# Seven half-size products in place of eight in the up projection of a SwiGLU layer, and full-height second products in the mixer

## The chip, the core and the metric

The kernel runs on one core of a Trainium2 chip. The metric is the device time of one launch in microseconds (us). The core has a matrix engine (PE, with its weight loads shown as PEld), three engines for vectors (DVE, ACT, POOL) and 16 DMA engines fed from queues, of which SP's carries nearly all weight loads here.

## The reference, cut to what matters

Two layers, each a half-step feed-forward layer, a mixer (attention, a gated linear recurrence and RWKV-7, merged by gates) and a second feed-forward layer, all in float32 with 512 tokens of 1024 channels; `D_FF` is 2816.

```python
def _swiglu(h, w_up, w_down):
    u, gte = _split(h @ w_up, [D_FF, D_FF])
    return (jax.nn.silu(u) * gte) @ w_down

for l in range(DEPTH):
    ...
    y = 0.5 * g1[:, None, :] * _swiglu(h, ffn_up[l, 0], ffn_down[l, 0])
    ...
    y = g2[:, None, :] * _mixer(h, w_in[l], ...)
    ...
    y = 0.5 * g3[:, None, :] * _swiglu(h, ffn_up[l, 1], ffn_down[l, 1])
```

## The kernel before

**Numbers.** PE multiplies in the type fp32r. To keep float32 accuracy every operand is held as two fp32r tiles, `hi` (a copy rounded to fp32r, made by ACT) and `lo` (the rest, made by a subtraction), and each product is three: hi·hi, hi·lo and lo·hi (`mm3`, lines 201 to 203). `split_w` (line 187) makes the two tiles of a weight, 128x1024 a time: ACT at line 194, and the subtraction at line 196 on DVE, or on POOL where `on_pool` is set (in the mixers, and in the first chunk of every feed-forward layer but the first). The activations of a layer lie split in `hhi` and `hlo` (1024 channels as 8 blocks `k` of 128, by 512 tokens).

**A feed-forward layer** (`ffn`, line 458) goes through the 2816 hidden channels in 22 blocks of 128, in chunks of 4, 4, 4, 5 and 5 blocks (`CHUNKS`). For a block it loads 128 columns of the u half and 128 of the gate half, splits both, and multiplies: 2 halves x 8 `k` x 3 = 48 products of 128x512 into two PSUM banks. `up_act` (line 477) then takes silu(u) on ACT, multiplies by the gate half on DVE (line 480) and splits the result (`split_act`: ACT line 649, DVE line 650). After the blocks of a chunk come its down products (24 of 128x512 for each block; `token_major`), whose sums are added to the residual by DVE at lines 553 and 554. The first three blocks of a layer are done in two halves of 256 tokens, the first half while the last tokens of the layer before are still being normed. Beside it run the steps of the next layer's conditioning (`ada`, a `bg_step` after each block: four 128x512 multiply-adds on DVE, lines 282 and 284). The last feed-forward layer has none.

**Slots.** Split weights rotate through 4 + 5 slots of `hi` and `lo` (`WBASE`, `WEXT`), in a layer's last chunk through the 4 alone; raw weights through 3 slots of 128x2048 numbers.

**In the mixer** some second products take only 64 of the 128 rows of the array: the `lo` part of a weight or a key against the `hi` half of an operand whose other 64 rows hold its `lo` part: line 705 (`lora`), line 1056 (attention scores) and line 1252 (the gates of the recurrence). They stand between products of all 128 rows.

**Order.** The program is written as generators; a scheduler then orders the instructions of each engine when the kernel is built, and each engine runs its list strictly in that order, waiting on semaphores.

Of the kernel before, what the change touches and what calls it, by code (L numbers as in the profile page):

```python
# [32 lines left out]
WEXT = {"raw": 0, "hi": 5}  # L33
# [26 lines left out]
class Trunk:  # L60
    def __init__(self, ctx, tc, a, out):
# [4 lines left out]
        self.on_pool = False  # L66
# [183 lines left out]
    def ada(self, l, v, q, dst, mul=1.0):  # L250
# [6 lines left out]
        if self.starting:  # L257

            ps = self.ps("c")
            for kk in range(0, KB, 4):  # L260
                rs = [self.we.tile([P, 2, 512], F32, tag=tag, bufs=WEXT["hi"], name=self.nm("ada")) for tag in ("hi", "lo")]
# [173 lines left out]

    def token_major(self, acc, lhs, rhs, first, last, kbs, by_tile, then=None, halves=False):
# [21 lines left out]
    def ffn(self, l, f, sub, nxt, begin):  # L458
# [3 lines left out]
        with self.tc.tile_pool(name=self.nm("ffn"), bufs=1, reuse_waits="tile") as fp:  # L462
# [13 lines left out]

            def up_act(pss, hi, lo):
                su = fp.tile([P, S], F32, tag="su", bufs=2, name=self.nm("su"))
                nc.scalar.activation(su, pss[0], AF.Silu)
                nc.vector.tensor_tensor(out=su, in0=pss[1], in1=su, op=ALU.mult)  # L480
                self.split_act(su, hi, lo)
# [6 lines left out]
            for c, n in enumerate(CHUNKS):  # L488
# [7 lines left out]
                if c == 0:  # L496
# [12 lines left out]
                    for i, (pss, ws) in enumerate(todo):  # L509
                        if not begin:  # L510
                            up_mm(pss, ws, 256, S)
                        up_act(pss, ahi[:, i, :], alo[:, i, :])
                    j = 3
                    self.wmode = "all"
                while j < n:
                    m = min(2, n - j)
                    for i, r in enumerate(up_load(b0 + j, m)):
                        pss = [self.ps("g"), self.ps("g")]
                        with later(c):
                            ws = [self.split_w(w) for w in r]  # L520
                        up_mm(pss, ws, 0, S)
                        up_act(pss, ahi[:, j + i, :], alo[:, j + i, :])
# [158 lines left out]
    def rwkv_head(self, l, p, rp):  # L681
# [19 lines left out]
        def lora(i):  # L701

            ps, r = self.ps("r"), ROWS[i]
            mm(out=ps, lhsT=whi[:, i, :], rhs=self.lora[:, i, :], start=True, stop=False)
            mm(out=ps, lhsT=wlo[r, i, :], rhs=self.lora[r, i, :], start=False, stop=True)
# [270 lines left out]
    def fox_prelude(self, l, ap):  # L976
# [3 lines left out]
        fb = ap.tile([P, H], F32, tag="fbias", name=self.nm("fbias"))  # L980
# [14 lines left out]
        room = ap.tile([P, S], F32, tag="et", bufs=2, name=self.nm("room"))  # L995
# [17 lines left out]
    def fox_pair(self, l, p, ap):  # L1013
# [8 lines left out]
        kl = ap.tile([P, S], F32R, tag="kl", bufs=1, name=self.nm("kl"))  # L1022
# [7 lines left out]
        for hh, r in enumerate(ROWS):  # L1030
            nc.scalar.activation(ks[r, hh, :], ps[r], AF.Copy)
            nc.vector.tensor_tensor(out=kl[r], in0=ps[r], in1=ks[r, hh, :].bitcast(F32), op=ALU.subtract)
# [14 lines left out]
        for i in range(NT):  # L1047
            n = i * P
            es = []
            for hh, fb in enumerate(fbs):  # L1050
                r = slice(64 * hh, 64 * hh + 64)
# [4 lines left out]
                mm(out=sc[:, 0 : n + P], lhsT=qs[r, hh, n : n + P], rhs=kl[r, 0 : n + P], start=False, stop=True)  # L1056
# [132 lines left out]
    def fox(self, l):  # L1189
        with self.tc.tile_pool(name=self.nm("at"), bufs=1, reuse_waits="tile") as ap:  # L1190
            prelude, pair = self.fox_prelude(l, ap), self.fox_pair(l, 0, ap)
# [7 lines left out]
    def lru(self, l):  # L1199
# [3 lines left out]
        with self.tc.tile_pool(name=self.nm("lru"), bufs=1, reuse_waits="tile") as lp:  # L1203
# [7 lines left out]
            for jj in range(0, KB, 2):  # L1211
                pair = []
                for j in (jj, jj + 1):
# [36 lines left out]
                    for n, r in enumerate(ROWS):  # L1250
# [247 lines left out]
```

## Time and profile before

| | us |
|---|---|
| median of 3 runs | 3123.97 (3116.07 to 3132.67) |
| the profiled execution | 3126.28 |
| its span in the trace | 3124.5 |
| PE busy | 2969.8 (95%) |
| DVE busy | 1876.6 (60%) |
| ACT busy | 1142.3 (37%) |
| POOL busy | 550.3 (18%) |
| granted TensorE clock, mean | 0.983 |

The four feed-forward layers lie at about 0 to 411, 1176 to 1565, 1565 to 1920 and 2725 to 3124 us, the two mixers between. Matmuls are pipelined: a row's own duration is longer than the distance to the next row, and it is the distance that PE's time is made of. A DVE or POOL row that had to wait for something inside the engine shows it as a longer duration, not as idle time before it.

### The profile page before, as it was taken

The numbers are of one execution on the slowest core, as the hardware profiler recorded it, in microseconds if no ns is written. First come the engines' busy times: TensorE is split into PE (matmuls) and PEld (weight loads), VectorE is DVE, ScalarE is ACT, GpSimd is POOL, SyncE is SP. The second block draws the span as 40 slices with busy tenths as digits, with TensorE's granted clock in tenths as the row PEclk, the third lists the DMA queues.
The fourth block names the chain that finished last, engine by engine and source line by source line (L and its number), as shares of the span: only waits on it lengthen the run. The fifth ranks groups of instructions, "written<-read, shape, count | busy, mean of one in ns | idle before, by whom it ended". The sixth has DMA issues, their size and how long they took to land. (4 is left out here: it accounts for less than half of the span.)

```text
span 3124.5 us, 39347 instructions
## 1 busy us (share of the span) xinstructions
PE 2969.8 (95%) x15330; PEld 2340.9 (75%) x15330; DVE 1876.6 (60%) x3534; ACT 1142.3 (37%) x1699; POOL 550.3 (18%) x375
## 2 busy tenths in 40 slices
PE   7999998999999999999999999889989899999998
PEld 5888876666666788888888888766667667788887
DVE  6655567556774756555565546666676756655435
ACT  4222252333545625222252213423335455342212
POOL 0000142223232004000130001422332320130000
PEclk9999999899999999999999999999999999999999
DMA  8634333233332453534434334433233324632321
GB/s 278 222 110 153 103 125 91 70 100 87 105 107 65 137 196 96 177 111 152 128 105 144 114 111 143 122 98 95 83 86 101 104 68 145 206 105 95 97 68 61
DMA packets 389402, 372.17 MB, mean 119 GB/s; under 512 B 54964, under 2 KB 318544, under 8 KB 389216
## 3 DMA queue, kind: packets, MB, share of 16 engines
q1 hardware_dynamic: 377048, 350.14, 36.6%
q10 hardware_dynamic: 12168, 19.53, 1.7%
q8 instruction: 120, 1.97, 0.3%
q14 instruction: 66, 0.54, 0.1%
HBM read 347.54 MB, written 22.09 MB: 118 GB/s over the span
## 5 line engine op out<-in xcount | busy, mean ns | idle before, releaser
L194 ACT ACTIVATE hi<-raw 128x1024 fp32r<-128x1024 f32 (+1 forms) x460 | 469.2, 1028 | 1259.3 <-PE pg L202 514.0
L196 POOL TENSOR_TENSOR lo<-raw,hi 128x1024 fp32r<-128x1024 f32 x164 | 407.0, 2485 | 1709.0 <-ACT hi L194 1662.5
L201 PE MATMUL pg<-hhi,hi 128*128 128x512 f32 (+1 forms) x1744 | 685.1, 396 | 11.8 <-DVE T L866 3.3
L202 PE MATMUL pg<-hlo,hi 128*128 128x512 f32 (+1 forms) x1744 | 677.5, 392 | 2.9 <-DVE nm L343 2.9
L203 PE MATMUL pg<-hhi,lo 128*128 128x512 f32 (+1 forms) x1744 | 678.9, 393 | 0.0
L196 DVE TENSOR_TENSOR lo<-raw,hi 128x1024 fp32r<-128x1024 f32 (+1 forms) x296 | 342.3, 1164 | 302.6 <-ACT hi L194 297.3
L201 PEld LDWEIGHTS pg<-hhi,hi 128*128 128x128 f32 x1744 | 332.4, 191 | 89.6 <-issue 14.4
L202 PEld LDWEIGHTS pg<-hlo,hi 128*128 128x128 f32 x1744 | 332.4, 191 | 69.0 <-issue 8.8
L203 PEld LDWEIGHTS pg<-hhi,lo 128*128 128x128 f32 x1744 | 331.9, 191 | 69.0 <-issue 4.7
L202 PE MATMUL pr<-hlo,hi 128*128 128x512 f32 (+1 forms) x816 | 299.3, 367 | 5.1 <-DVE nm L343 2.9
L201 PE MATMUL pr<-hhi,hi 128*128 128x512 f32 (+1 forms) x816 | 300.5, 369 | 2.2 <-ACT hhi L397 2.2
L203 PE MATMUL pr<-hhi,lo 128*128 128x512 f32 (+1 forms) x816 | 299.9, 368 | 0.0
L284 DVE SCALAR_TENSOR_TENSOR acc<-raw,cact,acc 128x512 f32<-128x512 f32 x224 | 187.7, 838 | 47.2 <-DMA raw<-in_ada_w_dram 42.7
L202 PEld LDWEIGHTS pr<-hlo,hi 128*128 128x128 f32 x816 | 154.1, 189 | 34.2 <-issue 7.4
L201 PEld LDWEIGHTS pr<-hhi,hi 128*128 128x128 f32 x816 | 154.0, 189 | 28.3 <-ACT hhi L397 2.6
L203 PEld LDWEIGHTS pr<-hhi,lo 128*128 128x128 f32 x816 | 154.2, 189 | 27.5 <-issue 0.2
L352 POOL TENSOR_TENSOR rstd<-var,mhalf 128x1 f32<-128x1 f32 x48 | 30.2, 629 | 469.8 <-DVE var L351 460.7
L201 PE MATMUL ps<-hi,ahi 128*128 128x512 f32 x264 | 103.5, 392 | 0.0
L203 PE MATMUL ps<-hi,alo 128*128 128x512 f32 x264 | 103.3, 391 | 0.0
L202 PE MATMUL ps<-lo,ahi 128*128 128x512 f32 x264 | 103.1, 391 | 0.0
L480 DVE TENSOR_TENSOR su<-pg,su 128x512 f32<-128x512 f32 x42 | 28.9, 688 | 117.2 <-PE pg L203 117.0
L480 DVE TENSOR_TENSOR su<-pr,su 128x512 f32<-128x512 f32 x42 | 28.9, 689 | 112.6 <-PE pr L203 108.6
(442 smaller groups left out, 4952.7 us busy)
## 6 DMA issues: line engine op xcount, KB each, us to landing
raw<-in_ffn_up_dram SPq DMA_DIRECT2D x70, 1024.0 KB
raw<-in_w_in_dram SPq DMA_DIRECT2D x132, 512.0 KB
raw<-in_ada_w_dram SPq DMA_DIRECT2D x64, 1024.0 KB
raw<-in_ffn_down_dram SPq DMA_DIRECT2D x40, 1024.0 KB
raw<-in_ffn_up_dram SPq DMA_DIRECT2D x36, 512.0 KB
gspill<-gate ACTq DMA_DIRECT2D x48, 256.0 KB
gate<-gspill SPq DMA_DIRECT2D x48, 256.0 KB
ada<-in_ada_w_dram SPq DMA_DIRECT2D x16, 512.0 KB
```

What stands on the lines that cost most here:

```text
L194: self.nc.scalar.activation(hi, v, AF.Copy)
L196: eng.tensor_tensor(out=lo, in0=v, in1=hi.bitcast(F32), op=ALU.subtract)
L201: mm(out=ps, lhsT=lhi, rhs=rhi, start=start, stop=False, **kw)
L202: mm(out=ps, lhsT=lhi, rhs=rlo, start=False, stop=False, **kw)
L203: return mm(out=ps, lhsT=llo, rhs=rhi, start=False, stop=stop, **kw).ins
L284: nc.vector.scalar_tensor_tensor(out=acc, in0=r[:, i, :], scalar=c, in1=acc, op0=ALU.mult, op1=ALU.add)
L352: nc.gpsimd.tensor_tensor(out=r, in0=v, in1=self.mhalf, op=ALU.pow)
L480: nc.vector.tensor_tensor(out=su, in0=pss[1], in1=su, op=ALU.mult)
```

## The change

**Seven products.** For a block, the stacked weights (u columns over gate columns) are cut in halves of the 1024 channels, `k1` and `k2`, and the tokens in halves of 256. Eight products of one weight quarter by one activation quarter become seven, between sums of quarters (Strassen's scheme in Winograd's form). One of the seven is 4 `k` x 3 = 12 products of 128x256. It is done for all blocks but the first three of a layer, 19 of 22, so 76 in the kernel.

- `combine` (once a layer, after the first of these three blocks): six activation sums and the splits of three of them into tiles `T`; DVE, POOL and ACT, on 128x1024 each. The tiles of the norm's weights and of the gate (`lng`, `lnb`, `gb`) serve as room. `combined` overwrites one quarter of `hhi` and `hlo` by the fourth sum, when the first three blocks have read it.
- `seven_weights` (each block): four sums of 128x512 on POOL into two tiles `s`; then three splits of 128x1024 (u, and the two tiles of sums) and one of 128x512 (`g2hi`, `g2lo`, one buffer).
- `seven` (each block): seven products into 256 columns of three PSUM banks x, y, z. Four ACT copies (lines 504, 508, 510, 512) take out sums between products, and the next product into the same bank waits for the copy; DVE adds at lines 506 and 515, POOL at line 513; silu at line 516; the two multiplications at lines 518 and 519.
- Slots: 4 + 3 of `hi` and `lo`.

**Full-height second products.** Lines 705, 1056 and 1252 now use all 128 rows; `kl` gets two planes with the other 64 rows set to zero once a layer.

```diff
-WEXT = {"raw": 0, "hi": 5}
+WEXT = {"raw": 0, "hi": 3}
...
+    def combine(self):
...
+        v(out=a, in0=hi[1], in1=lo[1], op=ALU.add)
+        g(out=b, in0=hi[3], in1=lo[3], op=ALU.add)
+        v(out=c, in0=a, in1=hi[0], op=ALU.subtract)
+        v(out=c, in0=c, in1=lo[0], op=ALU.subtract)
+        g(out=d, in0=b, in1=a, op=ALU.subtract)
+        v(out=a, in0=b, in1=c, op=ALU.subtract)
+        for i, t in enumerate((a, c, d)):
+            nc.scalar.activation(self.T[i][0], t, AF.Copy)
+            (g if i == 2 else v)(out=self.T[i][1], in0=t, in1=self.T[i][0].bitcast(F32), op=ALU.subtract)
+        g(out=b, in0=hi[2], in1=a, op=ALU.subtract)
+        g(out=b, in0=b, in1=lo[2], op=ALU.add)
+        self.late = b
...
+        t = nc.gpsimd.tensor_tensor
+        k1, k2 = slice(0, 4), slice(4, 8)
+        t(out=a[:, k2], in0=g[:, k1], in1=g[:, k2], op=ALU.add)
+        t(out=a[:, k1], in0=a[:, k2], in1=u[:, k1], op=ALU.subtract)
+        t(out=b[:, k1], in0=u[:, k1], in1=g[:, k1], op=ALU.subtract)
+        t(out=b[:, k2], in0=u[:, k2], in1=a[:, k1], op=ALU.subtract)
+        ws = []
+        for v in (u, a, b):
+            hi, lo = self.split_w(v)
+            ws += [(hi[:, k], lo[:, k]) for k in (k1, k2)]
+        hi, lo = (self.we.tile([P, 4, P], F32R, tag=n, name=self.nm(n)) for n in ("g2hi", "g2lo"))
+        self.split_act(g[:, k2], hi, lo)
...
+        product(0, x, True)
+        act(s1, x, AF.Copy)
+        product(1, y, True)
+        v(out=s1, in0=s1, in1=y, op=ALU.add)
+        product(2, x, False)
+        act(s2, x, AF.Copy)
+        product(3, z, True)
+        act(p5, z, AF.Copy)
+        product(4, x, False)
+        act(u3, x, AF.Copy)
+        nc.gpsimd.tensor_tensor(out=u3, in0=u3, in1=p5, op=ALU.add)
+        product(5, z, False)
+        v(out=s2, in0=s2, in1=z, op=ALU.add)
+        act(su, su, AF.Silu)
+        product(6, x, False)
+        v(out=s1, in0=s1, in1=x, op=ALU.mult)
+        v(out=s2, in0=s2, in1=u3, op=ALU.mult)
...
-                        pss = [self.ps("g"), self.ps("g")]
-                        with later(c):
-                            ws = [self.split_w(w) for w in r]
-                        up_mm(pss, ws, 0, S)
-                        up_act(pss, ahi[:, j + i, :], alo[:, j + i, :])
+                        up_pair(r, ahi[:, j + i, :], alo[:, j + i, :])
...
-            mm(out=ps, lhsT=wlo[r, i, :], rhs=self.lora[r, i, :], start=False, stop=True)
+            mm(out=ps, lhsT=wlo[:, i, :], rhs=self.lora[:, i, :], start=False, stop=True)
...
-                mm(out=sc[:, 0 : n + P], lhsT=qs[r, hh, n : n + P], rhs=kl[r, 0 : n + P], start=False, stop=True)
+                mm(out=sc[:, 0 : n + P], lhsT=qs[:, hh, n : n + P], rhs=kl[:, hh, 0 : n + P], start=False, stop=True)
...
-                        nc.tensor.matmul(out=pg[n], lhsT=wlo[r, n, :], rhs=xs[r, n, :], start=False, stop=True)
+                        nc.tensor.matmul(out=pg[n], lhsT=wlo[:, n, :], rhs=xs[:, n, :], start=False, stop=True)
```

**DVE, first feed-forward layer, fourth chunk.** Before, from the end of one block to the end of the next but one (`su` a block's result, `lo` a weight's rest, `acc` the conditioning):

```order
L650 TENSOR_TENSOR alo_1857<-su_1989,ahi_1856 128x512
L196 TENSOR_TENSOR lo_2235<-raw_2228,hi_2234 128x1024
L480 TENSOR_TENSOR su_2060<-pr_2003,su_2060 128x512
L196 TENSOR_TENSOR lo_2241<-raw_2238,hi_2240 128x1024
L650 TENSOR_TENSOR alo_1857<-su_2060,ahi_1856 128x512
L196 TENSOR_TENSOR lo_2393<-raw_2386,hi_2392 128x1024
L282 TENSOR_SCALAR acc_2522<-raw_2523,cact 128x512
```

After, one block of that chunk (`s` the tiles of weight sums, `hc` the room of u3):

```order
L506 TENSOR_TENSOR su_2576<-su_2576,pr_2578 128x256
L196 TENSOR_TENSOR lo_2826<-s_2815,hi_2825 128x1024
L286 TENSOR_SCALAR acc_2808<-raw_2809,cact 128x512
L288 SCALAR_TENSOR_TENSOR acc_2808<-raw_2809,cact,acc_2808 128x512
L196 TENSOR_TENSOR lo_2830<-s_2816,hi_2829 128x1024
L288 SCALAR_TENSOR_TENSOR acc_2808<-raw_2809,cact,acc_2808 128x512
L515 TENSOR_TENSOR su_2576<-su_2576,pg_2579 128x256
L288 SCALAR_TENSOR_TENSOR acc_2808<-raw_2809,cact,acc_2808 128x512
L519 TENSOR_TENSOR su_2576<-su_2576,hc_2580 128x256
L518 TENSOR_TENSOR su_2576<-su_2576,pr_2577 128x256
```

One operation on PSUM for a block (L480) has become three (L506, L515, L518), each behind subtractions for later blocks.

**ACT at the same place.** Before, around one block:

```order
L194 ACTIVATE hi_2234<-raw_2228 128x1024
L479 ACTIVATE su_2060<-pr_2002 128x512
L194 ACTIVATE hi_2240<-raw_2238 128x1024
L649 ACTIVATE ahi_1856<-su_2060 128x512
L194 ACTIVATE hi_2392<-raw_2386 128x1024
```

After:

```order
L194 ACTIVATE hi_2825<-s_2815 128x1024
L508 ACTIVATE su_2576<-pr_2577 128x256
L194 ACTIVATE hi_2829<-s_2816 128x1024
L510 ACTIVATE hc_2580<-pg_2579 128x256
L512 ACTIVATE hc_2580<-pr_2577 128x256
L516 ACTIVATE su_2576<-su_2576 128x512
L740 ACTIVATE g2hi_2703<-raw_2683 128x512
```

The copies that free a bank for the next product (L508, L510, L512) now stand between the splits for the block after next.

**POOL, start of the second feed-forward layer.** Before, the end of the norm and then the subtractions of the fourth block and of the first down weights:

```order
L352 TENSOR_TENSOR rstd_9616<-var_9614,mhalf 128x1
L352 TENSOR_TENSOR rstd_9654<-var_9652,mhalf 128x1
L352 TENSOR_TENSOR rstd_9668<-var_9666,mhalf 128x1
L196 TENSOR_TENSOR lo_10129<-raw_10126,hi_10128 128x1024
L196 TENSOR_TENSOR lo_10133<-raw_10126,hi_10132 128x1024
```

After, from the last weight sum of the fourth block on (`lo_11235` and `lo_11243` are that block's, `lo_11367` to `lo_11377` belong to the down weights):

```order
L480 TENSOR_TENSOR s_11229<-raw_11225,s_11228 128x512
L452 TENSOR_TENSOR lnb_10404<-hhi,hlo 128x1024
L455 TENSOR_TENSOR gb_10402<-lnb_10404,lng_10403 128x1024
L460 TENSOR_TENSOR lnb_10404<-hhi,lng_10403 128x1024
L461 TENSOR_TENSOR lnb_10404<-lnb_10404,hlo 128x1024
L196 TENSOR_TENSOR lo_11235<-raw_11225,hi_11234 128x1024
L459 TENSOR_TENSOR T_11102<-gb_10402,T_11101 128x1024
L196 TENSOR_TENSOR lo_11367<-raw_11360,hi_11366 128x1024
L196 TENSOR_TENSOR lo_11373<-raw_11370,hi_11372 128x1024
L196 TENSOR_TENSOR lo_11377<-raw_11370,hi_11376 128x1024
L196 TENSOR_TENSOR lo_11243<-s_11229,hi_11242 128x1024
```

Five activation sums have come in ahead of the fourth block's subtractions, and three down weights ahead of its last.

## Rows read from the trace of the kernel before

**Rows 1.** The page: busy time, share and instructions of the engines.
```profile
PE 2969.8 (95%) x15330; PEld 2340.9 (75%) x15330; DVE 1876.6 (60%) x3534; ACT 1142.3 (37%) x1699; POOL 550.3 (18%) x375
```
**Rows 2.** Windows, two feed-forward stretches: length, PE, PEld, DVE, ACT, POOL busy, clock, DMA share, GB/s.
```profile
1260.00:1540.00 280.00, 280.00 (x1230) 228.16 (x1229) 156.83 (x202) 70.31 (x84) 0.00 (x0) 1.00 0.41 135
2800.00:3090.00 290.00, 290.00 (x1261) 236.85 (x1260) 122.72 (x148) 70.84 (x85) 0.00 (x0) 1.00 0.25 80
```
**Rows 3.** Timeline of PE, products of 256 columns: start, duration, line, tiles.
```profile
419.83 0.28 PE L201 MATMUL pg<-hhi,hi 128*128 128x256 f32 x1
...
425.48 0.28 PE L201 MATMUL pc<-hhi,hi 128*128 128x256 f32 x1
...
1238.01 0.28 PE L201 MATMUL pr<-hhi,hi 128*128 128x256 f32 x1
...
1240.85 0.28 PE L202 MATMUL pc<-hlo,hi 128*128 128x256 f32 x1
```
**Rows 4.** Groups of instructions: count | busy us, mean ns | idle before.
```profile
L196 DVE TENSOR_TENSOR lo<-raw,hi 128x1024 fp32r<-128x1024 f32 x264 | 320.4, 1222 | 299.3 <-ACT hi L194 294.1
L480 DVE TENSOR_TENSOR su<-pg,su 128x512 f32<-128x512 f32 x42 | 28.9, 688 | 117.2 <-PE pg L203 117.0
L918 DVE COPY UX<-pc 64x128 f32<-64x128 f32 x64 | 18.4, 288 | 38.8 <-PE pc L916 38.0
L194 ACT ACTIVATE hi<-raw 128x1024 fp32r<-128x1024 f32 x428 | 449.1, 1057 | 1206.5 <-PE pg L202 487.2 <-PE pr L202 326.3 <-PE ps L203 152.9
L479 ACT ACTIVATE su<-pg 128x512 f32<-128x512 f32 x42 | 24.4, 581 | 9.6 <-PE pg L203 5.0 <-DMA vrow<-in_lru_ga_b_dram 4.6
L196 POOL TENSOR_TENSOR lo<-raw,hi 128x1024 fp32r<-128x1024 f32 x164 | 407.0, 2485 | 1709.0 <-ACT hi L194 1662.5 <-PE pg L203 16.7 <-PE pc L916 9.0
L1272 POOL TENSOR_TENSOR bout<-i,ge 128x512 f32<-128x512 f32 x16 | 21.9, 1366 | 139.3 <-DVE i L1271 139.3
```
**Rows 5.** One line's instructions, DVE line 650, 100 to 390 us: ns min/median/max.
```profile
L650 DVE TENSOR_TENSOR alo<-su,ahi x18: 673/684/1985, 121.9 to 380.9; 128x512 fp32r<-128x512 f32 x18
```
**Rows 6.** Timeline of DVE and POOL around the start of the second feed-forward layer.
```profile
1204.13 2.58 POOL L196 TENSOR_TENSOR lo<-raw,hi 128x1024 fp32r<-128x1024 f32 x1 [0.97 <-ACT hi L194]
1204.40 3.39 DVE L399 TENSOR_TENSOR hlo<-hf,hhi 128x1024 fp32r<-128x1024 f32 x1
1224.50 1.22 DVE L399 TENSOR_TENSOR hlo<-hf,hhi 128x1024 fp32r<-128x1024 f32 x1 [1.19 <-ACT hhi L397]
1237.57 8.13 POOL L196 TENSOR_TENSOR lo<-raw,hi 128x1024 fp32r<-128x1024 f32 x3 [2.73 <-ACT hi L194]
1237.71 0.68 DVE L480 TENSOR_TENSOR su<-pg,su 128x512 f32<-128x512 f32 x1
1239.09 1.52 DVE L650 TENSOR_TENSOR alo<-su,ahi 128x512 fp32r<-128x512 f32 x1 [0.70 <-ACT ahi L649]
```
**Rows 7.** Groups on DVE in 1300 to 1545 us: conditioning, residual.
```profile
L284 DVE SCALAR_TENSOR_TENSOR acc<-raw,cact,acc 128x512 f32<-128x512 f32 x32 | 24.0, 751 | 5.5 <-DMA raw<-in_ada_w_dram 4.6
L554 DVE SCALAR_TENSOR_TENSOR xt<-xt,tmp 128x512 f32<-128x512 f32 x24 | 15.3, 679 | 0.0
```
**Rows 8.** Windows, start of the second feed-forward layer, columns as in rows 2.
```profile
1225.00:1250.00 25.00, 25.00 (x200) 24.10 (x199) 9.61 (x10) 12.97 (x16) 15.36 (x6) 1.00 0.38 125
```
**Rows 9.** Mixer on PE: counts by line, four products in time, then a mixer's window.
```profile
L705 PE MATMUL pr<-lora,w x16: 492/498/793, 459.5 to 2426.3; 64*128 64x512 f32 x16
L1056 PE MATMUL ps<-kl,q x64: 323/435/792, 503.6 to 2330.6; 64*128 64x128 f32 x16, 64*128 64x256 f32 x16, 64*128 64x384 f32 x16, 64*128 64x512 f32 x16
L1252 PE MATMUL ps<-xs,wlo x32: 491/498/793, 819.1 to 2591.3; 64*128 64x512 f32 x32
818.70 0.51 PE L1251 MATMUL ps<-xs,whi 128*128 128x512 f32 x1
820.41 0.51 PE L201 MATMUL pg<-hhi,hi 128*128 128x512 f32 x1
411.00:1176.00 765.00, 713.51 (x3973) 534.62 (x3972) 490.64 (x1093) 319.54 (x522) 200.86 (x138) 0.96 0.38 110
```

## What the change does to the time, told ahead

> **What bounds the kernel now.** I read three views, in this order. First the busy times of the page [rows 1]: PE has work for 2969.8 us of a span of 3124.5, and the other engines look far from full. Then the windows over the feed-forward layers [rows 2]: in both stretches PE is busy for the whole length (280 of 280 us, 290 of 290) at the full granted clock, so there the time is the number of products times their distance, 280/1230 = 0.2277 us for 128x512 (290/1261 = 0.230 in the last layer). Nothing that waits there ends late, and fewer columns through PE is time gained, as long as the others keep up. In these stretches DVE is busy for 157 of 280 us, or 123 of 290 in the last layer, and POOL for none. Last the mixer's window [rows 9]: PE 713.5 of 765 us, not full, so work taken from PE there comes back in part only.
>
> **PE in a block.** The old block is 48 x 0.2277 = 10.93 us. The new one has seven products of 12 matmuls, 84 of 256 columns. Two stretches of such matmuls show their distance [rows 3]: from 419.83 to 425.48 lie 48 of them, 0.1177 us each, and from 1238.01 to 1240.85 lie 25, 0.1136. I take 0.1165: 84 x 0.1165 = 9.79 us (9.54 to 9.89). Gain: 1.14 us a block (1.04 to 1.39). Times 76 blocks: **-87 us** (-79 to -106). It is less than an eighth of the block (1.37 us), since two matmuls of 256 columns take a little longer than one of 512.
>
> **The preparation of a block, on DVE and POOL.** Before, a block cost DVE two subtractions of 1.22, if they were its own, one multiplication of 0.69 and one split of 0.68 [rows 4, 5]. Now DVE has three subtractions of 128x1024 (3 x 1.22), one of 128x512 for `g2lo` (0.68), the split of the result (0.68), the product at line 519 (two SBUF operands, 256 wide, some 0.4) and three operations of 256 columns on PSUM, between 0.29 (128 columns of 64 partitions) and 0.69 (512 columns) each [rows 4], some 0.45. POOL has four sums of 128x512; its nearest row is 1.37 [rows 4], so about 4 x 1.3, and the sum for `u3` of 256 columns, about half of that: 5.8 us. ACT has three splits of 1.06 and ten smaller ones, below 8 us [rows 4]. Each engine by itself has room beside 9.79 us, DVE less of it with the conditioning.
>
> But DVE and POOL are not independent [rows 6]. At 1204.40 a DVE subtraction of two SBUF tiles that takes 1.22 elsewhere (at 1224.50) took 3.39: a POOL subtraction ran from 1204.13 to 1206.71, and DVE's ended 1.08 after it. At 1239.09 a split took 1.52 beside POOL's three, where the median is 0.684 [rows 5]; the multiplication at 1237.71, with one operand in PSUM, took its usual 0.68 beside POOL. So an operation of DVE with two SBUF operands and one of POOL go one after the other. The Trainium skill, page "SBUF — State Buffer", section "🔬 SBUF: two separate sides", says the same as a rule: DVE and GpSimd share a pair of ports under an exclusive lock, held for the whole instruction by whoever starts first. The rows above agree; by engines counted apart the blocks below would wait for nothing but the order inside them, and by the rule this change, which gives POOL its first work in these stretches, fills one shared resource.
>
> The time of that resource for four blocks and their down products: for a block 3 x 1.22 + 0.68 + 0.68 + 0.4 = 5.4 of DVE and 5.8 of POOL, 11.2; its down weight 1.22; so 4 x 12.4 = 49.7. The residual takes eight of line 554, 0.68 each [rows 7], about 5. The conditioning shows 24.0 us of line 284 in 245 us [rows 7], about 6 in such a group. Sum **60.7 us**. PE after the change: 4 x 9.79 + 96 x 0.2277 = 61.1; before: 4 x 10.93 + 21.9 = 65.6. So in three of the layers the pair must be in use for 99% of the time if PE is not to wait; in the last, without conditioning, for 90%. Weights can be prepared ahead by 7/3 = 2.3 blocks, which carries work from the blocks into the down products.
>
> **Waits inside a block.** Each copy out of a bank has one product, 12 x 0.1165 = 1.4 us, until that bank is needed again. A copy of 256 columns takes some 0.4 (between 0.29, DVE's small copy at line 918, and 0.58, ACT's 512 columns at line 479 [rows 4]); when a split of 1.06 stands ahead of it, 1.46, which is about 0.1 to 0.2 us late with the signals. At the block's end the chain line 515, silu (0.58), line 518 takes 0.45 + 0.58 + 0.45 = 1.5 and must be through before the second product of the next block, 2.8 us after the fifth sum is there: 1.0 to 1.3 us of room. One `lo` of 1.22 ahead of line 515 on DVE uses it up; that `lo` waiting for a POOL sum as well makes the chain about 1.1 us late. So a wait of 0.2 to 1.3 us by the order alone; I take 0.2 and half of the 1.1, **0.7 us**, where the pair is not full (the 19 blocks of the last layer: +13). In the other 57 blocks I take the pair as used for at most 94%: 60.7/0.94 = 64.6, less 61.1, over four blocks, **0.87 us**: +49. No row shows that share. Its ends are 100%, with the order's own 0.2 left, and 86% (70.6 us, 2.4 a block). In favour of the good end: at the start of the second layer [rows 8] DVE and POOL show 12.97 and 15.36 us in 25, more than the stretch together because waiting lies inside the rows, and PE is busy for all 25. Blocks together: **+62 us** (+15 to +150).
>
> **Start of a layer.** `combine` puts ten operations of 128x1024 or so on POOL and DVE. In the second layer, and the two others whose first weights are POOL's, activation sums stand on POOL's queue ahead of the fourth block's `lo`, and three down weights ahead of its last. The last `hlo` of the norm ends at 1225.72 [rows 6]; PE then has the three second halves, 3 x 48 x 0.1165 = 17 us, and needs the last of those `lo` some 6 us later, at +23. POOL has ten operations of 2.4, 24 us, plus its waits for DVE, near 10: +31 to +34. So 8 to 11 us late there, about 6 at the two others, where more comes early: **+22 us** (0 if the sums go in before the norm ends, 45 if each start costs 11). The sums that overwrite `hhi` come when the first blocks have read it; I cost them nothing beyond this.
>
> **Mixer.** Four products on PE at lines 1251 and 1252, two of each, take 818.70 to 820.41, 1.71 us [rows 9], where four of 0.2277 would take 0.91: 0.4 us for each product of 64 rows. With 32 of line 1252, 16 of 705 and 64 of 1056 (mostly narrower, so 0.3): 13 + 6 + 19 = 38 us as the most. Since PE has gaps there (51 of 765 us), I take **-30** (-12 to -41). The planes set to zero cost a few operations of a layer, which lie beside the first heads.
>
> **The sum.** 3126.3 - 87 + 62 + 22 - 30 = 3093.3 for the profiled execution, which stands 2.3 above the median: **3090 us** is my forecast (by its own terms 3060 to 3108).
>
> **Rivals.** *The cover holds.* The order's 0.2 a block is all, the starts cost 5, the mixer gives 38: 3124 - 87 + 15 + 5 - 38 = 3019. For it: PE never waited in these stretches and the stretch of rows 8 was as crowded; against: 99% of the pair leaves no room for waits of either queue.
>
> *Gain and costs cancel.* 1.2 us a block, the order's bad end, in the three layers and 1.0 in the last (68 + 19 = 87), 28 at the starts, 30 in the mixers: 3124 - 87 + 87 + 28 - 30 = 3122.
>
> *The pair of DVE and POOL sets the pace: slower.* POOL's sums and DVE's subtractions exclude each other, each queue also waits for DMA and for ACT's `hi`, and while one waits the other is often not ready. At 88% a group takes 69.0 us, 1.97 a block: 57 x 1.97 + 13 = 125, so 3124 - 87 + 125 + 22 - 30 = 3154. It decides from 1.47 us a block on (57 x 1.47 + 13 = 97 uses up 87 + 30 - 22 = 95), that is 67.0 us a group, 90.6% in use. For it: rows 6, and the 60.7 us; against: the waits of both queues can overlap, and weights are ready 2.3 blocks ahead.
>
> *The seven do not do what they say* in the sense that 256 columns cost 0.13 instead of 0.1165 (84 x 0.13 = 10.92, no gain): rows 3 speak against it, in two stretches of up to 48. I give it no share of its own.
>
> **How the numbers follow.** Forecast 0.38; cover holds 0.17; cancel 0.19; the pair sets the pace 0.26. Of the forecast nearly all lies more than 0.5% below 3124 (under 3108), which is about what a measurement of this kernel can tell from no change: faster 0.54, same 0.20 and slower 0.26. The range takes in the cover holding to 3010, and the pair at 86% (57 x 2.37 + 13 = 148, 3177) to 3175; without the slower rival it would be 3010 to 3125.
>
> **What would show it.** Right or wrong by step: the distance of matmuls inside a product of twelve (0.1165), and the time from one block's first to the next one's (10.5 to 10.7, against 9.8 if the cover holds and 11.8 if the pair sets the pace); idle time of PE ahead of the lines 201 to 203, which was nil, now released by ACT at lines 504 to 512 (the order), by DVE at 518 (the chain) or by DVE at 196 (the pair: weights not ready); rows of DVE at line 196 above 1.22 and of POOL above 1.3, for the lock, and whether the last layer, which has no conditioning, gains most; PE idle at about 25 us after the norm in the second layer, behind POOL; in the mixer a distance of 0.23 for line 1252's successor, and whether a mixer's span falls by the 15 us taken. Wrong altogether it would be if POOL's sums of weights took far more than 1.3 us, or if DVE did not wait for them.

## The result: 3290.5 us, 5.3% slower

| | before | after |
|---|---|---|
| median | 3122.97 (4 runs, 3116.07 to 3132.67) | 3290.49 (4 runs, 3282.66 to 3296.20) |
| span of the profiled execution | 3124.5 | 3290.2 |
| granted clock, mean | 0.983 | 0.960 |

The ratio is 1.0532, 95% interval 1.0496 to 1.0568. I had forecast 3090 with a range of 3010 to 3175: wrong in sign, and outside the range.

The page of after, the row that answers to [rows 1] (busy us, share, instructions):

```profile
PE 2931.0 (89%) x18066; PEld 2464.8 (75%) x18066; DVE 2326.4 (71%) x3939; ACT 1381.4 (42%) x2171; POOL 1196.2 (36%) x782
```

PE is busy for 39 us less than before, in a span that is 166 us longer. No engine is full. Windows of after, one in the second feed-forward layer and one in the last (columns as in [rows 2]):

```profile
1320.00:1620.00 300.00, 266.39 (x1799) 246.74 (x1798) 228.64 (x276) 115.07 (x178) 117.77 (x81) 0.95 0.36 118
2960.00:3250.00 290.00, 269.18 (x1857) 248.06 (x1856) 205.50 (x236) 122.95 (x190) 120.77 (x81) 0.99 0.28 91
```

Where [rows 2] had PE busy for the whole length, 34 of 300 us and 21 of 290 are now gaps. In the first window DVE's and POOL's rows add up to 346 us of 300: some of DVE's work may lie beside POOL's, but part of this sum is waiting inside the rows.

Cut at the ends of the norms and at the first and last product of each chunk's down weights, the two traces differ so:

| part, sums over the layers | before | after | |
|---|---|---|---|
| norm to first down product, four layers | 128 | 190 | +61 |
| the 18 later blocks of each layer | 812 | 912 | +100 |
| down products and the rest | | | +15 |
| norms | | | +19 |
| two mixers | 1511 | 1481 | -30 |

**What a wait looks like.** PE in the second layer of after (start, duration, line, tiles, idle time before and what ended it):

```profile
1375.32 0.28 PE L201 MATMUL pg<-hhi,hi 128*128 128x256 f32 x1
1375.43 0.28 PE L202 MATMUL pg<-hlo,hi 128*128 128x256 f32 x1
...
1375.90 0.28 PE L203 MATMUL pg<-hhi,lo 128*128 128x256 f32 x1
1379.02 0.58 PE L201 MATMUL pr<-hhi,g2hi 128*128 128x256 f32 x1 [2.83 <-ACT hc L512]
1379.40 0.42 PE L202 MATMUL pr<-hlo,g2hi 128*128 128x256 f32 x1
1379.61 0.42 PE L203 MATMUL pr<-hhi,g2lo 128*128 128x256 f32 x1
```

ACT and POOL at that moment, same columns:

```profile
1373.45 0.38 ACT L510 ACTIVATE hc<-pg 128x256 f32<-128x256 f32 x1 [1.11 <-PE pg L203]
1377.64 1.06 ACT L194 ACTIVATE hi<-s 128x1024 fp32r<-128x1024 f32 x1 [3.80 <-POOL s L478]
1378.60 0.37 ACT L512 ACTIVATE hc<-pr 128x256 f32<-128x256 f32 x1
```
```profile
1373.85 1.29 POOL L477 TENSOR_TENSOR s<-raw 128x512 f32<-128x512 f32 x1 [7.54 <-DMA raw<-in_ffn_up_dram]
1375.10 1.29 POOL L479 TENSOR_TENSOR s<-raw,raw 128x512 f32<-128x512 f32 x1
1376.34 1.26 POOL L478 TENSOR_TENSOR s<-s,raw 128x512 f32<-128x512 f32 x1
```

PE waits for the copy at line 512; that copy stands on ACT behind the split of a tile of weight sums for a later block; the split waits for POOL's sums; and these waited 7.54 us for their raw weights, whose two loads SyncE issued at 1362.42 and 1368.68 us, both times released by DVE. Following each wait of PE back in this way, 98 of the 183 us of waits in the four layers' bodies (from the end of a layer's norm on) end with a copy behind such a split, 34 with line 518 behind DVE's queue.

After the gap the matmuls are 0.21 us apart instead of 0.117. Windows of after before, right behind and after the gap; the seventh figure is the granted clock:

```profile
1364.00:1376.00 12.00, 12.00 (x104) 11.90 (x102) 6.39 (x9) 6.05 (x11) 3.06 (x3) 1.00 0.76 251
1379.00:1383.50 4.50, 4.48 (x19) 4.17 (x20) 4.15 (x6) 2.57 (x4) 4.38 (x3) 0.64 0.00 0
1384.00:1396.00 12.00, 12.00 (x53) 9.71 (x53) 9.06 (x9) 2.13 (x2) 3.69 (x3) 1.00 0.36 115
```

The clock falls from its 2.4 GHz level to the 1.2 GHz one behind a wait and comes back some microseconds later (0.64 is the mean of a stretch that holds both). The distances above the usual ones, added over the bodies of the four layers, make 67 us (under 4 before). Waits and low clock together are 250 us there; with the 87 us that the blocks save taken off, some 163 are left, which is what the table's first two lines have (61 + 100).

### The profile page after: what moved, and what is told of

It is laid out like the page before. It is cut to its first block, busy times and chain, and to the rows that moved or that the text cites. A ratio compares the mean times of both kernels' runs of the same rounds, so it can differ in the third digit from the quotient of the medians.

```text
span 3290.2 us, 46569 instructions
## 1 busy us (share of the span) xinstructions
PE 2931.0 (89%) x18066; PEld 2464.8 (75%) x18066; DVE 2326.4 (71%) x3939; ACT 1381.4 (42%) x2171; POOL 1196.2 (36%) x782
## 5 line engine op out<-in xcount | busy, mean ns | idle before, releaser
L203 PE MATMUL pg<-hhi,lo 128*128 128x512 f32 (+1 forms) x1592 | 568.8, 361 | 0.0
L194 ACT ACTIVATE hi<-s 128x1024 fp32r<-128x1024 f32 x152 | 160.7, 1058 | 395.8 <-PE ps L203 159.0
L196 DVE TENSOR_TENSOR lo<-s,hi 128x1024 fp32r<-128x1024 f32 x146 | 202.4, 1392 | 149.5 <-ACT hi L194 148.7
L477 POOL TENSOR_TENSOR s<-raw 128x512 f32<-128x512 f32 x76 | 123.4, 1624 | 359.1 <-DMA raw<-in_ffn_up_dram 177.2
L201 PE MATMUL pr<-hhi,hi 128*128 128x256 f32 (+1 forms) x664 | 195.7, 295 | 32.5 <-DVE su L518 19.3
L513 POOL TENSOR_TENSOR hc<-hc 128x256 f32<-128x256 f32 x76 | 92.9, 1222 | 349.6 <-ACT hc L512 337.2
L202 PE MATMUL pr<-hlo,hi 128*128 128x256 f32 (+1 forms) x664 | 193.8, 292 | 5.1 <-DVE nm L347 4.5
L203 PE MATMUL pr<-hhi,lo 128*128 128x256 f32 (+1 forms) x664 | 192.8, 290 | 3.2 <-POOL lo L196 3.2
L201 PE MATMUL pg<-T,hi 128*128 128x256 f32 x448 | 133.0, 297 | 28.1 <-ACT su L504 16.3
L201 PE MATMUL pr<-T,hi 128*128 128x256 f32 x464 | 135.5, 292 | 18.2 <-ACT su L508 13.0
L203 PE MATMUL pr<-T,lo 128*128 128x256 f32 x464 | 134.1, 289 | 5.3 <-POOL lo L196 5.3
```

Source lines behind the costliest of these rows:

```text
L194: self.nc.scalar.activation(hi, v, AF.Copy)
L196: eng.tensor_tensor(out=lo, in0=v, in1=hi.bitcast(F32), op=ALU.subtract)
L201: mm(out=ps, lhsT=lhi, rhs=rhi, start=start, stop=False, **kw)
L202: mm(out=ps, lhsT=lhi, rhs=rlo, start=False, stop=False, **kw)
L203: return mm(out=ps, lhsT=llo, rhs=rhi, start=False, stop=stop, **kw).ins
L477: t(out=a[:, k2], in0=g[:, k1], in1=g[:, k2], op=ALU.add)
```

## Experiments

A time without a ratio is that of one run, beside runs of before on the same chip (medians 3121 to 3126 us); the runs of the changed kernel itself spread over 14 us.

**One part alone, and the order.** `mixer_only` is before with lines 705, 1056 and 1252 changed, and what they need: the two planes of `kl` with their zeros, and room for them.

> The kernel before with the full-height second products of the mixer alone, no seven products. Theory: in the changed kernel the time from the end of one norm to the start of the next shrank by 24.4 us in the first mixer and by 6.0 in the second, and that is this edit's; so alone it gives 3123 - 30 = 3093 us (1% faster), and the feed-forward layers keep their 0 us of PE waits. Rival: the shorter first mixer is a side effect of what the seven products move (weights and conditioning already done), and the edit alone is worth 0 to 12 us: 3111 to 3123.

Measured: 3094.67 us, ratio 0.9899 (0.9877 to 0.9922). Between the norms the mixers went from 760.1 to 739.5 us and from 751.1 to 738.6. The theory holds: this half of the change is worth 31 us. The whole loss, then, some 196 us (3290.5 less 3094.7), belongs to the seven products and the slots and tiles that changed with them.

My first theory for it was the queue on ACT shown above. Three kernels on it:

```diff
# order
+            behind = self.tc.issue_after(self.last_u3) if self.last_u3 is not None and v is not u else nullcontext()
+            with behind:
                 hi, lo = self.split_w(v)
...
-        act(u3, x, AF.Copy)
+        self.last_u3 = act(u3, x, AF.Copy).ins
# sums_unread
-        for v in (u, a, b):
+        for v in (u, g, g):
# no_sums: the same, and
-        t(out=a[:, k2], in0=g[:, k1], in1=g[:, k2], op=ALU.add)
...
-        t(out=b[:, k2], in0=u[:, k2], in1=a[:, k1], op=ALU.subtract)
```

> The changed kernel, with one order forced: on ACT the splits of the two tiles of weight sums stand behind the copy of u3 (line 512) of the block before, so that no copy that frees a bank waits behind a split whose sum POOL has not made. Nothing is left out. Theory (the queue): in the four feed-forward bodies 98 of the 183 us in which PE waits end with a copy that stood behind such a split, and the low clock after the waits costs a third on top; with the copies ahead these go, and the time falls by 60 to 120 us, to 3170 to 3230. Rival (the pair of DVE and POOL sets the pace): the same operations need the same shared time, the waits come back at line 518 or as late weights, and the time stays within 25 us of 3290.

> The changed kernel, with the splits reading the raw gate weights in place of the two tiles of weight sums: POOL still makes all four sums of a block, but nothing reads them (the products are of the wrong weights, so part of the computation is changed). The load on POOL and on what it shares with DVE is the same; only the wait of ACT for POOL's sums is gone. Theory (the queue): 80 to 130 us less, 3160 to 3210. Rival (the pair): within 25 us of 3290.

> As sums_unread, and the four POOL sums of each block are left out as well (part of the computation is left out): wait and load both gone, 76 x 5.2 = 395 us of POOL less. Theory (the queue): only a little better than sums_unread, by up to 30 us, 3140 to 3200. Rival (the pair): here the gain comes, 100 us or more below sums_unread.

Measured: 3263.9, 3260.8 and 3113.2 us. The queue theory falls: with the copies ahead, or with nobody waiting for the sums, only 27 and 30 us come back; PE's waits take other last links (over the whole trace, line 518's multiplication ends 68 us of them in either kernel, 38 in after). Leaving the sums out brings 148 more. It is their being done that costs.

**What about the sums costs.** `port_only` and `port_free` take sums_unread and change what POOL does; `fill_read` and `port_read` do the same in the changed kernel, so that the splits read POOL's tiles and hold POOL back as the sums do.

```diff
# port_only, port_read
+        h = [self.hhi[:, 4:8, P * i : P * i + P].bitcast(F32) for i in range(2)]
+        for v, k in ((a, k2), (a, k1), (b, k1), (b, k2)):
+            t(out=v[:, k], in0=h[0], in1=h[1], op=ALU.add)
# port_free, fill_read
+        for v in (a, a, b, b):
+            nc.gpsimd.memset(v, 0.0)
+            nc.gpsimd.memset(v[:, 0:2], 0.0)
```

> As sums_unread (the splits read raw gate weights, nothing reads POOL's sums), but POOL's four sums of a block have parts of the layer's resident activations as operands in place of the raw weights: the same POOL time and the same exclusion with DVE, but no raw slot is held for POOL any more. Lock theory (POOL's sums cost because DVE's operations on two SBUF operands wait for them, and they for DVE's): stays near sums_unread, 3235 to 3265. Rival 1 (raw slots come free late because POOL reads them): falls to near no_sums, 3110 to 3150. Rival 2 (POOL's own queue is full): as the lock theory here.

> As port_only, with POOL's sums replaced by fills with zero that read nothing: for each block 4 x (128x1024 + 128x256), by the rows of fills (0.95 for 128x1024) about 4 x 1.25 = 5 us, as long as the sums. POOL's queue is as long; only the exclusion with DVE is gone, if a fill does not take part in it. Lock theory: near no_sums, 3110 to 3150. Rival 2 (POOL's own queue is full, or its instructions stand in the way of its other work): near sums_unread, 3235 to 3265.

> The changed kernel with POOL's four sums of a block replaced by fills with zero into the same tiles, read by the same splits (so six of the quarter products use zero weights; part of the computation is changed). POOL's time for a block stays about 5 us, ACT still waits for POOL's tiles, and the fills are held back by the two tiles as the sums are; what goes is the exclusion with DVE (a fill does not lengthen DVE's rows) and the wait of POOL for the raw weights. Lock theory: POOL's sums cost through the exclusion; 3130 to 3180. Rival (a slow engine in the middle of ACT's queue is enough): 3230 to 3290.

> As fill_read (3131), with POOL's fills replaced by four sums of 128x512 of parts of the resident activations, into the same tiles, read by the same splits (six of the quarter products use these in place of weight sums; part of the computation is changed). Against the changed kernel only the operands differ: POOL doesn't wait for the raw weights and holds none of their slots. Against fill_read only the kind of POOL's operation differs: it reads. Lock theory (the exclusion of DVE and POOL is the cost): 3240 to 3290. Rival (POOL's sums cost because they wait for raw weights that come late and keep their slots): 3130 to 3160.

Measured: 3431.2, 3205.3, 3131.3 and 3269.7 us. The last two differ in whether POOL's operation reads: 138 us. They also differ in the weights that come of it, zeros in fill_read; no_sums, with weights that are not zero, lies near it at 3113, so the zeros are not what makes it fast. Their groups on DVE and POOL (count | busy, mean ns | idle before), fill_read first:

```profile
L196 DVE TENSOR_TENSOR lo<-s,hi 128x1024 fp32r<-128x1024 f32 x146 | 186.8, 1281 | 113.1 <-ACT hi L194 112.0 <-PE pr L203 0.7 <-PE pg L203 0.3
L478 POOL MEMSET s<- 128x1024 f32 x304 | 291.2, 960 | 506.4 <-DVE lo L196 469.0 <-PE ps L378 28.5 <-PE pc L378 0.2
L479 POOL MEMSET s<- 128x256 f32 x304 | 94.8, 314 | 14.3
```

and port_read:

```profile
L196 DVE TENSOR_TENSOR lo<-s,hi 128x1024 fp32r<-128x1024 f32 x146 | 214.4, 1473 | 90.1 <-ACT hi L194 89.5
L479 POOL TENSOR_TENSOR s<-hhi 128x512 f32<-128x512 f32 x304 | 483.6, 1612 | 522.5 <-DVE lo L196 489.2 <-ACT hhi L401 31.6 <-PE ps L378 1.1
```

Fills take POOL 386 us and leave DVE's subtractions near the 1222 of [rows 4]; sums, 1.26 us when alone, take 1612 ns each and DVE's subtractions 1473. This is the exclusion of [rows 6], now between two kernels whose POOL operations differ in reading. The Trainium skill, page "SBUF — State Buffer", section "🔬 SBUF: two separate sides", has it as a rule: a DVE operation with two SBUF inputs excludes only a GpSimd operation that reads SBUF; these two runs agree. That the raw weights' slots are held for POOL (the rival in port_read) is worth some 20 us: 3290 against 3270.

The same window of three kernels and after shows it as products done, the count behind PE's busy time; after, port_read, fill_read and (below) sums_dve:

```profile
1320.00:1560.00 240.00, 212.42 (x1411) 196.02 (x1410) 179.50 (x215) 93.25 (x142) 94.42 (x65) 0.96 0.36 121
```
```profile
1320.00:1560.00 240.00, 215.86 (x1434) 197.62 (x1434) 189.02 (x219) 94.40 (x143) 95.62 (x65) 0.97 0.38 127
```
```profile
1320.00:1560.00 240.00, 233.28 (x1622) 213.74 (x1621) 174.66 (x253) 107.02 (x163) 84.55 (x121) 1.00 0.42 140
```
```profile
1320.00:1560.00 240.00, 235.70 (x1611) 214.82 (x1610) 212.50 (x324) 109.12 (x168) 25.96 (x20) 1.00 0.41 132
```

The other two missed their numbers because nothing held POOL back in them. In port_only the sums of many blocks ran end to end at a layer's start (POOL is busy for all of 1300 to 1400 us). DVE's subtractions in 1300 to 1500 us of it:

```profile
L196 DVE TENSOR_TENSOR lo<-raw,hi 128x1024 fp32r<-128x1024 f32 x21 | 74.3, 3547 | 43.5 <-ACT hi L194 43.5
```

Each took 3.5 us instead of 1.22: the lock theory's direction, and more than it had said. In port_free it was another operation that was shut out; that is told in the last section.

**Sums on DVE, and the conditioning.**

```diff
# sums_dve
-        t = nc.gpsimd.tensor_tensor
+        t = nc.vector.tensor_tensor
# light_cond
-                else:
+                elif i == 0:
                     nc.vector.scalar_tensor_tensor(out=acc, ...
```

> The changed kernel with the four sums of a block on DVE in place of POOL; nothing is left out. DVE takes about 0.68 for such an operation, so 2.7 us of DVE instead of 5.2 of POOL: the time that both share falls from 11.2 to 8.7 us a block, but DVE alone has about 9.5 us a block, with conditioning and residual some 61 us in four blocks and their down products, as much as PE. Lock theory: 3180 to 3240, better than the changed kernel by 50 to 110. Rival (DVE becomes the bound): 3260 to 3340.

> The changed kernel with three of every four multiply-adds of the background conditioning left out (the modulation is then wrong; part of the computation is left out): some 190 operations of two SBUF operands on DVE, 0.75 us alone, 144 us, all in the first three feed-forward layers. Lock theory (the shared time of DVE and POOL sets the pace): each of these three layers, which now lose 50 us against before, comes to the fourth layer's loss of 26 or below, together 60 to 100 us less: 3190 to 3230. Rival (order alone; DVE's share does not pace): 10 to 40 us less, 3250 to 3280.

Measured: 3127.8 and 3263.3 us. Moving the sums brings 163 us, more than the lock theory said, and DVE, busy for 212.5 of 240 us in the window above, is no bound: PE is busy for 235.7 of them. Light_cond came out at the rival's size: 27 us, not 60 to 100. The trace tells more. The later blocks of the first three layers are 46 us shorter than in after, while the first mixer is 11 us longer and the down products 10. So the load on the pair counts, but less than I had put it at: 192 operations, some 144 us, were gone. Why it matters no more than that is open; its loads were left in.

**Starts and norms.**

```diff
# late_start: block four of the first chunk (c is 0) as before
...
+                            pss = [self.ps("g"), self.ps("g")]
+                            with later(c):
+                                ws = [self.split_w(w) for w in r]
+                            up_mm(pss, ws, 0, S)
+                            up_act(pss, ahi[:, j + i, :], alo[:, j + i, :])
...
# dve_late: that, sums_dve, and
-        nc.gpsimd.tensor_tensor(out=u3, in0=u3, in1=p5, op=ALU.add)
+        v(out=u3, in0=u3, in1=p5, op=ALU.add)
# start_room: dve_late, and d, the room of one activation sum, no longer in the gate's tile
+        d = self.lp.tile([P, D], F32, tag="xn", bufs=2, name=self.nm("hd"))
# start_dve: start_room, and
-        v, g = nc.vector.tensor_tensor, nc.gpsimd.tensor_tensor
+        v = g = nc.vector.tensor_tensor
...
                     j = 3
+                    self.on_pool = False
# slots_only: before, with the last weights of the mixer's output from a pool of three, as in after, and
-WEXT = {"raw": 0, "hi": 5}
+WEXT = {"raw": 0, "hi": 3}
```

> The changed kernel, with the fourth block of each layer as before (eight half-size products' worth, 48 of 128x512), so that the activation sums and the weight sums need not be ready until the second chunk, some 33 us later; nothing is left out. Theory (the starts cost what the traces show, 61 us more than before over four layers from the end of the norm to the first down product, part of it the wait for POOL's late weights): 35 to 60 us less, 3230 to 3255, the four blocks themselves giving back 4 x 1.1. Rival (the wait moves to the second chunk, whose sums then queue behind the same work): within 20 us of 3290.

> The changed kernel with three edits, nothing left out: the four weight sums of a block on DVE (as in sums_dve, 3128), the sum for u3 on DVE too, and the fourth block of each layer as before (as in late_start). In sums_dve the blocks behind the first chunk already go at the pace the seven products allow (40.5 to 41.3 us for four, 45.5 before), and what is lost lies at the starts and in the norms behind a layer. Theory: the starts give back 10 to 15 us each, 3065 to 3090, ahead of both kernels and near or below the mixer edit alone (3095). Rival (DVE is the bound once it holds the sums, u3 and the splits): 3115 to 3140.

> dve_late (3116) with one edit, nothing left out: the activation sum that used the tile of the gate as room goes into one of the two tiles of weight sums. In dve_late's second layer SyncE held the reload of the gate for 41 us until POOL had read that room, and the raw weights of the second chunk, queued behind it, were issued up to 16 us late; PE then waited 9.5 us behind them. Theory (that queue costs at the starts): 10 to 14 us less in each of three layers, 3075 to 3095. Rival (the raw slots come free late by POOL's subtractions anyway): 3105 to 3120.

> start_room with two more edits, nothing left out: the activation sums all on DVE, and the subtractions of the fourth block's and the first chunk's down weights on DVE instead of POOL (POOL keeps those of the first three blocks). Theory (at the starts POOL's 2.4 us subtractions and sums, lengthened to 3.4 by DVE, free the raw slots late): the starts come to within 5 us of before each, 3055 to 3080, ahead of both kernels and of the mixer edit alone (3095). Rival (DVE has no room there, or the start is bound by something else): no better than start_room by more than 5 us.

> The kernel before with the slots of the changed one alone: 4 + 3 of hi and lo instead of 4 + 5 (with the last weights of the mixer's output taken from a pool of three, as in the changed kernel). Theory (the norms behind a layer and between layers, 16 to 19 us longer together in every kernel with the seven products, are longer because fewer split weights are ready behind them): the norms grow by 2 to 6 us each, 3130 to 3145. Rival (fewer slots cost nothing by themselves; the norms wait for the seventh block's work on DVE and POOL): 3118 to 3130.

Measured: 3281.4; 3116.39, ratio 0.9962 (0.9946 to 0.9979); 3118.6; 3070.03, ratio 0.9823 (0.9806 to 0.9839); and 3143.0 us. Putting the deadline off moves the wait instead of ending it (the rival of late_start): 3281.4 is hardly below the changed kernel's own runs (3282.7 to 3296.2), and in late_start's second layer PE now stands among the first chunk's down products:

```profile
1296.28 0.80 PE L201 MATMUL pr<-hi,ahi 128*128 128x512 f32 x1 [9.87 <-ACT su L571]
1307.34 0.80 PE L201 MATMUL pr<-hi,ahi 128*128 128x512 f32 x1 [9.42 <-DVE su L572]
```

Dve_late's time fell to its rival (DVE is the bound), but not for the rival's reason: start_dve puts still more on DVE and is faster. SyncE's queue behind the gate's reload was not what held the starts either (the rival of start_room). POOL was: taking its sums and its late subtractions out of them together brings the 49 us between start_room and start_dve; the two were not timed apart. Slots alone cost 19 us, as much as the norms have grown: from their first transposition to their last, the three norms behind the first three feed-forward layers are 14 us longer together in slots_only than in before, 16 in after. Start_dve, 1.8% faster than before, beats both kernels and mixer_only (0.9899); against the latter the seven products are worth some 25 us. A start, a chunk of four and a longer stretch of its second layer:

```profile
1209.00:1241.40 32.40, 32.40 (x239) 30.43 (x238) 29.39 (x31) 18.68 (x23) 0.00 (x0) 1.00 0.30 98
1327.65:1368.03 40.38, 40.38 (x349) 40.01 (x347) 35.86 (x58) 22.15 (x37) 0.00 (x0) 1.00 0.45 154
1290.00:1540.00 250.00, 246.93 (x1716) 226.21 (x1715) 217.58 (x341) 112.47 (x174) 6.91 (x4) 1.00 0.44 144
```

Four blocks between two chunks' down products take 40.38 us (45.46 before, 53.12 after), 1.27 us a block less than before, with PE busy throughout.

## Why the prediction was wrong, step by step

**PE in a block: right.** The mean distance of the 256-wide matmuls outside the waits and the low clock is 0.1167 us over 1565 of them in the second layer (forecast 0.1165), and where nothing waits a block gains what was forecast (1.14 us) and a little more (1.27 in the chunk of start_dve shown above; 1.0 over all of its 72 later blocks, some waits included).

**Waits of the blocks: the step that failed.** The term was the pair's use, put at 94% of the time. Forecast +62 us for 76 blocks, 0.8 each. The 72 blocks of the table's second line took 100 us more instead of 82 less: 2.5 us of waits each, 2.9 in the first three layers and 1.4 in the last. I had named the right pair and the right rows [rows 6], and added its load up correctly enough: the groups of after, the equals of [rows 4] and of the rows for 1.3 and 0.65,

```profile
L196 DVE TENSOR_TENSOR lo<-s,hi 128x1024 fp32r<-128x1024 f32 x146 | 202.4, 1392 | 149.5 <-ACT hi L194 148.7
...
L480 POOL TENSOR_TENSOR s<-raw,s 128x512 f32<-128x512 f32 x76 | 125.2, 1647 | 2.0
...
L513 POOL TENSOR_TENSOR hc<-hc 128x256 f32<-128x256 f32 x76 | 92.9, 1222 | 349.6 <-ACT hc L512 337.2 <-DVE lo L196 11.8
```

differ by waiting, apart from line 513 (forecast 0.65; its shortest is 0.73). But the 94% at which the pair could be used rested on no row. A chunk of four with its down products took 53.1 + 21.8 = 74.9 us in the second layer: my 60.7 us of load are 81% of it, below the 86% that I held to be the end. The six such chunks of the first three layers lie between 72 and 90%, those of the last layer at 79% (47.3 + 21.7 = 69.0 us, with 54.7 of load). So about 80% was to be had, and not the same in every chunk; what fixes it no run shows. In the chains followed above, an operation waits for the other engine's and then delays a split, a slot or a copy in a queue of fixed order. The sentence on rows 8, that PE was busy in a stretch as crowded, misled me: as I now read it (no run tests this), nothing on PE there depended on the next subtraction within a microsecond or two.

**The order inside a block** was priced at 0.2 to 1.3 us. A copy behind a split that itself waits for POOL was not among my cases, though the order shows it; by the runs it is a link, worth about 27 us when cut.

**The clock** had no term. Its 67 us are more than a third of the waits that set it off.

**Preparing ahead** by 2.3 blocks counted the split weights; the sums have two tiles, one block's worth, and the second half `g2` has one buffer, so POOL could not run further ahead than that. This is argued from the code and the trace; more tiles were not tried.

**Starts:** +22 forecast, +61 in the trace. The mechanism (POOL's queue) was right, as start_dve shows; the term was a third of the size. In the second layer the stretch from the norm to the first down product is 50.41 us with POOL busy for 46.68; the same stretch had been 32.40, all of it PE's:

```profile
1256.53:1306.94 50.41, 36.70 (x267) 35.60 (x266) 34.10 (x22) 20.06 (x26) 46.68 (x21) 0.83 0.22 74
```

**Norms:** forecast at nothing. They cost 19 us. The 4 + 3 slots stood in the change and I used them for the blocks alone; slots_only shows that they were enough.

**Mixer: right.** -30 forecast, -30 in the table, -31 alone. PE in after's first mixer, the place of [rows 9]:

```profile
854.72 0.50 PE L1345 MATMUL ps<-xs,whi 128*128 128x512 f32 x1
855.06 0.39 PE L1346 MATMUL ps<-xs,wlo 128*128 128x512 f32 x1
855.29 0.40 PE L1345 MATMUL ps<-xs,whi 128*128 128x512 f32 x1
855.53 0.39 PE L1346 MATMUL ps<-xs,wlo 128*128 128x512 f32 x1
855.75 0.40 PE L201 MATMUL pg<-hhi,hi 128*128 128x512 f32 x1
```

Four products take 1.03 us instead of 1.71, the later ones at 0.23 each.

**The sum.** Over the layers the table has +182 of waits and low clock less the 82 gained in 72 blocks, +61 at the starts, +15 at the down products and the rest, +19 in the norms and -30 in the mixers: +165, where the forecast had -33.

**The rival** in which the pair sets the pace had the sign, the place and a chance of 0.26; its price, 3154 and at most 3177, stopped short because it, too, hung on the unread share, and on the same starts, norms and clock.

## What to carry to other kernels

Before giving an idle engine work, look for what it shares: POOL was idle in these stretches, and the same sums on DVE, the busier engine, cost 163 us less. The load of a resource that two engines with fixed queues pass to and fro was not its price: here about 80% of it could be used. Where the load comes near the time at hand, count on waits, and on the low clock behind them, which made them a third dearer here. And a change in two halves is worth timing in halves: here one half gained 31 us and the other lost 196.

## What the runs showed of the hardware that was not expected

A fill on POOL doesn't disturb a DVE subtraction of two SBUF tiles, but fills that run end to end shut out a far smaller operation. DVE and POOL in the first layer of port_free:

```profile
120.92 1.20 DVE L196 TENSOR_TENSOR lo<-raw,hi 128x1024 fp32r<-128x1024 f32 x1
122.05 0.15 DVE L303 SCALAR_TENSOR_TENSOR gate<-ps,bias 128x8 f32<-128x8 f32 x1
122.14 0.27 DVE L675 COPY vcol<-ps 128x106 f32<-128x106 f32 x1
122.44 24.85 DVE L680 TENSOR_SCALAR omu<-vcol 128x14 f32<-128x14 f32 x1
...
147.38 3.49 DVE L196 TENSOR_TENSOR lo<-raw,hi 128x1024 fp32r<-128x1024 f32 x3
```
```profile
120.18 1.85 POOL L478 MEMSET s<- 128x1024 f32 x2
121.97 0.56 POOL L479 MEMSET s<- 128x256 f32 x2
...
145.42 1.84 POOL L478 MEMSET s<- 128x1024 f32 x2
```

The subtraction at 120.92 takes its 1.20 beside the fills. The operation at line 680, of 14 columns with one SBUF operand, takes 24.85 us, until the run of fills ends, and everything behind it on DVE waits. This is a large part of why port_free came out at 3205 instead of near 3113: PE stands for 24.7 and 23.3 us in this layer, and its last down product ends 44 us later than in no_sums. The section of the Trainium skill named above has a rule for it: of a DVE operation in a mode that uses both ports and any GpSimd operation, the one that starts first holds the ports for the whole instruction and the other is blocked. No run here shows the mode in which line 680 ran, and the rule speaks of one instruction, while line 680 waited through a run of them.

Products of 64 rows between products of 128 rows make themselves and their neighbours slow. At lines 1251 and 1252 of before each of the four took 0.42 to 0.44 us to the next, not only the two of 64 rows; at full height, in after's rows shown above, it is 0.23 for all but the first:

```profile
819.13 0.49 PE L1252 MATMUL ps<-xs,wlo 64*128 64x512 f32 x1
819.55 0.50 PE L1251 MATMUL ps<-xs,whi 128*128 128x512 f32 x1
819.99 0.49 PE L1252 MATMUL ps<-xs,wlo 64*128 64x512 f32 x1
```
